# A trunk kernel's head reordered: the first eight projection tiles by column halves

## The chip, the cores and the metric

One NeuronCore of a Trainium2 chip runs the whole kernel. The metric is the device time of one execution in microseconds, median over several runs.

## The reference, cut to what matters

One layer of a streaming encoder, in float32, 1024 tokens of width 1024. The head of it is this:

```python
c_act = jax.nn.silu(c)
mod = (c_act @ w_ada[i] + b_ada[i]).reshape(bsz, N_MOD, D_MODEL)[:, :, None, :]
shift1, scale1, gate1 = mod[:, 0], mod[:, 1], mod[:, 2]
u = rms_norm(x, ln1[i]) * (1.0 + scale1) + shift1
# in mixer_sublayer
proj = u @ w_in          # 11296 columns; the first 2048 are the gates gl
gl, cb, cc, cx, z, xbc, dt = jnp.split(proj, split_at, axis=-1)
g_conv, g_ssm = jnp.split(jax.nn.sigmoid(gl), 2, axis=-1)
```

Behind it come a gated convolution, an SSD scan in eight groups, three output projections, a squared-ReLU MLP and a last RMSNorm. The change touches only the way to u and the first eight of the 88 column tiles of `w_in`.

## The kernel before, in words

Everything is held transposed: channels on the 128 partitions, tokens along the free dimension. x and u are eight blocks j of 128 channels, each in two halves h of 512 tokens (`xt[j][h]`, `uh[j][h]`, `ul[j][h]`). A product in float32 is made of three: an operand is split into a high part (a cast to the type fp32r on ScalarE) and a low part (the difference, on VectorE), and high x high, high x low and low x high are added up in PSUM (`mm3`, three matmuls of 128 x 128 by 128 x 512). A plain tile f of `w_in` (128 columns, all 1024 inputs) thus costs 2 x 8 x 3 = 48 matmuls. From some point on the tiles go in pairs through a Strassen form (`strassen_pair`) with 7 products of 12 matmuls, 84 for two tiles; it needs sums and differences of quarter blocks of u (`tops_of`), each split again.

The head goes in this order. `crow` (c as a row) and `prm` (all small parameters) are loaded; c is spread over the partitions by a product with ones, and silu gives `cb`. SP loads the left halves of x, the two `wada` tiles of block 0 (rows of `w_ada` for scale and shift), the right halves of x, and weights of `w_in` and further `wada` tiles in turn. ScalarE squares x, VectorE adds the squares, `st` collects column sums on TensorE, `rsqrt_eps` gives the root on VectorE, and a product of ones with a diagonal (`sdg`) spreads it over the partitions as `rb0` and `rb1`, for both halves before any u is made. Then for each block j VectorE forms shift and scale by two multiply-and-reduce instructions over 1024 columns (`gemv`, line 294), one column `s1c`, both halves of x times scale times `rb`, and both low parts; ScalarE makes the two high parts (`shift_split`, line 106). TensorE runs four tiles (0 to 3) over block j as soon as it is there, in all eight PSUM banks.

When all blocks are done, the four tiles are passed through tanh (`gl_evac`) and stored to `gl_d`; tiles 4 and 5 go plainly; VectorE and ScalarE form the Strassen operands; `dt` (a product with 64 columns, line 397) follows, and then the Strassen pairs (6, 7), (8, 9) to (14, 15), and the rest of the kernel. `dt_chain` and the remaining 32 gemvs (`wada2`, loaded by POOL into one buffer `wv`, three beside each pair) lie beside those pairs.

The order on each engine is made by a planner from its own model of durations, in the order of the program as priority, except where `issue_after` puts an instruction behind another. DMA issues stand in the instruction streams of SP, ScalarE and POOL.

Of the kernel before, what the change touches and what calls it, by code (L numbers as in the profile page):

```python
# [35 lines left out]
NPAR = DSK + 16  # L36


def hybrid_trunk(tc, xT, par, hrows, crow, wada1, wada2, win, wdt, wco, wso, wo, wup, wdt_, wdn, out):
# [26 lines left out]
    s1c = cp.tile([P, 8], F32, name="s1c")
    s2c = cp.tile([P, 8], F32, name="s2c")
    g1c = cp.tile([P, 8], F32, name="g1c")
    cp.tile([P, 24], F32, name="lpad")
# [193 lines left out]
    crw = glp.tile([1, T], F32, name="crw", tag="glt")  # L263
    sp.dma_start(crw, crow)
    sp.dma_start(prm, par)
    for h in (0, 1):
        ps = mm.tile([P, H], F32, name="mm")
        pe.matmul(ps, lhsT=ones[0:1, :], rhs=crw[:, hs[h]], start=True, stop=True)
        act.activation(ct[:, hs[h]], ps, AF.Tanh, scale=0.5)
        stt(cb[:, hs[h]], ct[:, hs[h]], 1.0, ps, ALU.add, ALU.mult)  # L270
# [9 lines left out]
    for h in (0, 1):  # L280
        for k in range(KT):
            sp.dma_start(xt[k][h], xT[k, :, hs[h]])
        if h == 0:
            load_ada(0)
    raws = [load_raw(win[f]) for f in (0, 1)]
    load_ada(1)
    raws.append(load_raw(win[2]))
    raws.append(p0.tile([P, T], F32, name='wx', bufs=1))
    sp.dma_start(raws[3], win[3])

    wps = mm.tile([P, H], F32, name="mm")
# [5 lines left out]
    def warm(n, x_):  # L297
        for _ in range(n):
            pe.matmul(wps, lhsT=ones, rhs=x_, start=True, stop=True)

    warm(4, xt[0][0])
# [1 line left out]
    for h in (0, 1):
        acc = None
        for k in range(KT):
            sq = p0.tile([P, H], F32, name="ssq" if k else "sacc", bufs=4 if k else 2)
            act.activation(sq, xt[k][h], AF.Square)
            if k:
                tt(acc, acc, sq, ALU.add)
            else:  # L310
                acc = sq
        for j in range(4):
            pe.matmul(st[:, 4 * h + j:4 * h + j + 1], lhsT=acc[:, j * P:j * P + P], rhs=ones[:, 0:1],
                      start=h == j == 0, stop=True, skip_group_check=True)
# [1 line left out]
    r = rsqrt_eps(p0, st[:, 0:8], 1.0 / T, [P, 8], "nst")
    rbs = []
    for h in (0, 1):
        dg = p0.tile([P, 4, P], F32, name="sdg", bufs=1)
        rdy = tt(dg, ident.unsqueeze(1).broadcast_to([P, 4, P]),  # L320
                 r[:, 4 * h:4 * h + 4].unsqueeze(2).broadcast_to([P, 4, P]), ALU.mult)
# [1 line left out]
        pe.matmul(ps, lhsT=ones, rhs=dg.rearrange("p j t -> p (j t)"), start=True, stop=True)
# [4 lines left out]
    ws = []
    sps = [[None, None] for _ in range(4)]
    for h in (0, 1):  # L330
        for f in range(4):
            pl, nm = (mm, "mm") if f < 2 else (ps0, ("sx", "st")[h])
            sps[f][h] = pl.tile([P, H], F32, name=nm)
    for j in range(KT):
        if j > 1:
            load_ada(j)
        if j in (0, 1):
            with tc.issue_after(rdy.ins), (tc.issue_after(rbc.ins) if j else contextlib.nullcontext()):
                for f in range(2):
                    ws.append(load_w(win[2 * j + f], raws[2 * j + f]))  # L340
        with tc.issue_after(rdy.ins) if j else contextlib.nullcontext():
            gemv(wa[j, 1], 8 + j)
            gemv(wa[j, 0], j)
        stt(s1c[:, j:j + 1], mcol[:, 8 + j:9 + j], 1.0, prm[:, LN1 + j:LN1 + j + 1], ALU.add, ALU.mult)
        for h in (0, 1):
            x_ = xt[j][h]
            stt(x_, x_, s1c[:, j:j + 1], rbs[h], ALU.mult, ALU.mult)
            rdy = shift_split(uh[j][h], ul[j][h], x_, mcol[:, j:j + 1])
        if j == 0:
            continue  # L350
        for jj in ((0, 1) if j == 1 else (j,)):
            for h in (0, 1):
                for f in range(4):
                    mm3([sps[f][h]], ws[f][0][:, jj * P:jj * P + P], ws[f][1][:, jj * P:jj * P + P],
                        [uh[jj][h]], [ul[jj][h]], jj == 0, jj == KT - 1)
# [721 lines left out]
```

## Time and profile before

| what | value |
|---|---|
| median of 3 runs | 2122.07 us (2121.62 to 2123.22) |
| profiled execution | 2126.34 us, its span 2124.3 us |
| granted TensorE clock, mean of the span | 0.989 |
| TensorE busy | 2089.6 us (98%) |
| VectorE busy | 1474.3 us (69%) |
| ScalarE busy | 927.4 us (44%) |
| POOL busy | 152.3 us (7%) |

Times in profile lines are in us from the span's start. A line of a timeline gives start, duration, engine, source line, operation, out<-in, count, and in brackets the idle time before it with what ended it. L is a line of the kernel; line 44 is any tensor-tensor operation, 47 any scalar-tensor-tensor, 89 a weight load, 96 a cast to a high part, 106 the high part of u, 113, 114 and 116 the three matmuls of `mm3`, 147 a matmul of a Strassen pair.

### The profile page before, as it was taken

The numbers are of one execution on the slowest core, as the hardware profiler recorded it, in microseconds if no ns is written. First come the engines' busy times: TensorE is split into PE (matmuls) and PEld (weight loads), VectorE is DVE, ScalarE is ACT, GpSimd is POOL, SyncE is SP. The second block draws the span as 40 slices with busy tenths as digits, with TensorE's granted clock in tenths as the row PEclk, the third lists the DMA queues.
The fourth block names the chain that finished last, engine by engine and source line by source line (L and its number), as shares of the span: only waits on it lengthen the run. The fifth ranks groups of instructions, "written<-read, shape, count | busy, mean of one in ns | idle before, by whom it ended". The sixth has DMA issues, their size and how long they took to land.

```text
span 2124.3 us, 26250 instructions
## 1 busy us (share of the span) xinstructions
PE 2089.6 (98%) x9776; PEld 1705.5 (80%) x9776; DVE 1474.3 (69%) x2278; ACT 927.4 (44%) x1554; POOL 152.3 (7%) x242
## 2 busy tenths in 40 slices
PE   7999999999999999999999999999999999999998
PEld 4778888888888887888877888888888888888887
DVE  7866888665786757576786558845866665668674
ACT  4433333224565636364664231233544454544432
POOL 0000000000000000000000000011000001232213
PEclk8999999999999999999999999999999999999998
DMA  8226554223133223232337586453144347988932
GB/s 302 80 100 200 189 189 165 71 80 122 60 100 110 85 90 85 95 115 80 104 121 262 189 299 201 159 203 124 65 164 159 145 162 261 304 241 254 275 77 80
DMA packets 133617, 327.32 MB, mean 154 GB/s; under 512 B 12481, under 2 KB 47681, under 8 KB 131954
## 3 DMA queue, kind: packets, MB, share of 16 engines
q1 hardware_dynamic: 98978, 202.76, 29.4%
q0 software_dynamic: 22240, 87.04, 12.9%
q10 hardware_dynamic: 12272, 35.85, 4.3%
q8 instruction: 77, 1.26, 0.2%
q14 instruction: 50, 0.41, 0.1%
HBM read 253.05 MB, written 72.55 MB: 153 GB/s over the span
## 4 chain that ended last, share of the span: by engine, by line
PE 82%; issue 10%; DVE 4%; DMA 2%; POOL 1%; ACT 1%; SPq 0%; DVEq 0%; POOLq 0%; ACTq 0%
PE mm L147 21%; PE mm L116 15%; PE mm L113 15%; PE mm L114 15%; PE mm L971 9%; PE B L603 2%; PE B L608 1%; PE C L625 1%; DMA wv<-in_wada 1%; DVE wada L294 1%; PE A L580 1%; DMA x<-in_xT 1%; POOL wv L418 1%; DVE ul L47 1%; DVE x L47 0%
## 5 line engine op out<-in xcount | busy, mean ns | idle before, releaser
L113 PE MATMUL mm<-uh,whi 128*128 128x512 f32 x768 | 303.0, 398 | 3.7 <-ACT uh L106 3.2
L114 PE MATMUL mm<-ul,whi 128*128 128x512 f32 x768 | 304.8, 397 | 0.0
L147 PE MATMUL mm<-t,whi 128*128 128x512 f32 x944 | 290.5, 390 | 0.9 <-DVE cq L44 0.9
L116 PE MATMUL mm<-uh,wlo 128*128 128x512 f32 x768 | 246.4, 396 | 1.9 <-DVE wlo L44 1.9
L96 ACT CAST whi<-wraw 128x1024 fp32r<-128x1024 f32 x101 | 106.1, 1050 | 261.9 <-PE mm L114 219.9
L44 DVE TENSOR_TENSOR wlo<-wraw,whi 128x1024 fp32r<-128x1024 f32 (+1 forms) x167 | 186.6, 1118 | 37.4 <-ACT whi L96 31.3
L147 PEld LDWEIGHTS mm<-t,whi 128*128 128x128 f32 x944 | 176.9, 188 | 39.1 <-DVE cq L44 2.4
L971 PE MATMUL mm<-op,whi 128*128 128x512 f32 x672 | 207.2, 389 | 1.0 <-DVE y L47 0.9
L147 PE MATMUL mm<-t,wlo 128*128 128x512 f32 x472 | 183.0, 389 | 0.0
L113 PEld LDWEIGHTS mm<-uh,whi 128*128 128x128 f32 x768 | 144.5, 189 | 35.6 <-ACT uh L106 4.9
L116 PEld LDWEIGHTS mm<-uh,wlo 128*128 128x128 f32 x768 | 144.9, 189 | 32.2 <-DVE wlo L44 2.3
L114 PEld LDWEIGHTS mm<-ul,whi 128*128 128x128 f32 x768 | 145.0, 189 | 29.4 <-issue 0.9
L113 PE MATMUL mm<-ys,whi 128*128 128x512 f32 x384 | 148.9, 397 | 2.3 <-DVE gt L47 1.8
L44 DVE TENSOR_TENSOR wlo<-s,whi 128x1024 fp32r<-128x1024 f32 (+1 forms) x114 | 112.0, 995 | 54.4 <-ACT whi L152 53.6
L114 PE MATMUL mm<-ys,whi 128*128 128x512 f32 x384 | 149.1, 396 | 0.0
L971 PEld LDWEIGHTS mm<-op,whi 128*128 128x128 f32 x672 | 126.0, 188 | 28.1 <-ACT whi L957 1.3
L47 DVE SCALAR_TENSOR_TENSOR cacc<-raw,hw,cacc 128x1024 f32<-128x1024 f32 x96 | 122.9, 1280 | 27.6 <-ACT cacc L555 27.2
L147 PE MATMUL mm<-s,whi 128*128 128x512 f32 x448 | 138.3, 389 | 0.7 <-ACT cu L170 0.7
L971 PE MATMUL mm<-op,wlo 128*128 128x512 f32 x336 | 130.7, 389 | 0.0
L597 ACT ACTIVATE seg<-acb,acum 128x128 f32<-128x128 f32 x256 | 81.9, 392 | 98.7 <-PE B L603 88.6
L47 DVE SCALAR_TENSOR_TENSOR y<-mm,mcol,y 128x512 f32<-128x512 f32 (+1 forms) x100 | 69.4, 706 | 77.6 <-PE mm L971 39.4
L116 PE MATMUL mm<-ys,wlo 128*128 128x512 f32 x384 | 122.5, 394 | 0.0
(280 smaller groups left out, 4080.9 us busy)
## 6 DMA issues: line engine op xcount, KB each, us to landing
wraw<-in_win SPq DMA_DIRECT2D x87, 512.0 KB, 3.5
dr<-in_wdt_ SPq DMA_DIRECT2D x108, 256.0 KB, 5.8
op_d<-hp POOLq DMA_DIRECT2D x12, 1792.0 KB, 6.0
hr<-op_d POOLq DMA_DIRECT2D x42, 512.0 KB, 6.3
wv<-in_wada POOLq DMA_DIRECT2D x32, 512.0 KB, 3.8
acb<-ac_d SPq DMA_DIRECT2D x64, 256.0 KB, 4.5
wraw<-in_wup SPq DMA_DIRECT2D x32, 512.0 KB, 3.5
gt<-gl_d SPq DMA_DIRECT2D x24, 512.0 KB, 4.4
```

The lines of the kernel that those rows point to most:

```text
L44: return eng.tensor_tensor(out=o, in0=a, in1=b, op=op)
L47: return dve.scalar_tensor_tensor(out=o, in0=a, scalar=s, in1=b, op0=op0, op1=op1)
L96: act.copy(hi, raw)
L113: pe.matmul(o, lhsT=wh, rhs=h_, start=start, stop=False)
L114: pe.matmul(o, lhsT=wh, rhs=l_, start=False, stop=False)
L116: last_mm[0] = pe.matmul(o, lhsT=wl, rhs=h_, start=False, stop=stop)
L147: last_mm[0] = pe.matmul(o, lhsT=l_[:, s_], rhs=r_, start=first and k == j == 0, stop=k == 3 and j == 2, skip_group_check=True)
L294: return dve.tensor_tensor_reduce(out=w_, in0=w_, in1=cb, scale=0.5, scalar=prm[:, BADA + o:BADA + o + 1], op0=ALU.mult, op1=ALU.add, accu ...
L418: pool.dma_start(w_, wada2[i])
L597: act.activation(seg[:, r, :], acb[:, r, :], AF.Relu, bias=acum[:, c, hd:hd + 1], scale=-1.0)
L603: pe.matmul(Bk[o:o + 64, P * (r // 2):P * (r // 2) + P], lhsT=xd[:, r, :], rhs=seg[:, r, :], start=True, stop=True, skip_group_check=True)
L971: pe.matmul(o, lhsT=l_[:, c_], rhs=t[:, r_, k, :], start=first and k == j == 0, stop=k == 3 and j == 2, skip_group_check=True)
```

## The change

The first eight tiles are now all plain ones (the Strassen pairs begin at tile 8), and the head runs by halves: left half of the tokens for all eight tiles, then the right half. The order of all instructions of the head on TensorE, ScalarE, VectorE and SP is the order of the program text: each is chained to the one before it on its engine. In detail:

- Left x, two small `wk` tiles, the weights of tiles 0 to 2, two blocks of `wada`, then right x are loaded by SP. `wk` holds the weights of scale and shift for block 0 transposed, so that these two columns come from TensorE (`first_col`, 8 one-column products each) instead of two gemvs; c itself comes as a column, `ccol`.
- Weights of tiles 3 to 7 are loaded by POOL as a raw buffer (three of them) comes free.
- The low parts of tiles 6 and 7 are made by ScalarE writing the negated raw tile and a DMA of POOL that adds the raw tile from memory.
- The sum of squares and the root of the right half are made between the steps of the left half (`square(1, k)`, `sums(1)`, `root(1)`).
- In the left half, a step j is: scale gemv, low part of block j-1, x times scale, shift gemv, high part of block j. Weight tiles join as they are ready and catch up on earlier blocks. In the right half the tiles 4 to 7 follow block by block, and then 0 to 3 one after the other.
- Tanh and store of gl go by halves. `wada` has 4 buffers instead of 8. `dt_chain` stands at pair 10 instead of 8, and the gemvs beside pairs 12 and 14 are four each instead of three beside 10, 12 and 14.

The diff, cut to its core:

```diff
+    block = nc.cur_bb.bb.instructions
+    head = len(block)
...
+    rows_c = [mm.tile([P, H], F32, name="mm") for _ in (0, 1)]
+    wps = mm.tile([P, H], F32, name="mm")
+    def warm(n):
+        for _ in range(n):
+            pe.matmul(wps[:, 0:P], lhsT=ones, rhs=ones, start=True, stop=True)
+    warm(3)
     for h in (0, 1):
...
+        pe.matmul(rows_c[h], lhsT=ones[0:1, :], rhs=crw[:, hs[h]], start=True, stop=True)
     xt = [[xk[k % 4].tile([P, H], F32, name=f"x{k}{h}") for h in (0, 1)] for k in range(KT)]
     wa = {}
+    def load_x(h):
+        for k in range(KT):
+            sp.dma_start(xt[k][h], xT[k, :, hs[h]])
     def load_ada(j):
         for q in (1, 0):
-            wa[j, q] = p0.tile([P, T], F32, name="wada", bufs=8)
+            wa[j, q] = p0.tile([P, T], F32, name="wada", bufs=4)
...
+    whs, wls, raws = [], [], []
+    def load_f(f):
+        raws.append(wp.tile([P, T], F32, name="wraw", bufs=3))
+        (sp if f < 3 else pool).dma_start(raws[f], win[f])
+        pl, nh, nl, n = (wp, "whi", "wlo", None) if f < 4 else (p0w, "whx", "wlx", None)
+        whs.append(pl.tile([P, T], F32R, name=nh, bufs=n))
+        wls.append(pl.tile([P, T], F32R, name=nl, bufs=n))
+    def high(f):
+        act.copy(whs[f], raws[f])
+    def low(f):
+        tt(wls[f], raws[f], whs[f].bitcast(F32), ALU.subtract)
+    def low_by_dma(f):
+        act.mul(wls[f], raws[f], -1.0)
+        pool.dma_start(wls[f], win[f], accum_op=ALU.add)
     def gemv(w_, o):
         return dve.tensor_tensor_reduce(out=w_, in0=w_, in1=cb, scale=0.5, scalar=prm[:, BADA + o:BADA + o + 1],
...
+    load_x(0)
+    wk = []
+    for q in (1, 0):
+        wk.append(p0w.tile([P, T], F32, name=f"wk{q}", tag="whx"))
+        sp.dma_start(wk[-1], wadak[:, q])
+    for f in range(3):
+        load_f(f)
+    load_ada(1)
+    load_ada(2)
+    load_x(1)
+    def first_col(n):
+        for k in range(KT):
+            pe.matmul(cps[:, n:n + 1], lhsT=wk[n][:, k * P:k * P + P], rhs=ccol[:, k:k + 1], start=k == n == 0,
+                      stop=k == KT - 1, skip_group_check=True)
+    accs = {}
+    def square(h, k):
+        sq = p0.tile([P, H], F32, name="ssq" if k else "sacc", bufs=2 if k else 1)
+        act.activation(sq, xt[k][h], AF.Square)
+        if k:
+            tt(accs[h], accs[h], sq, ALU.add)
+        else:
+            accs[h] = sq
+    def scale_of(j):
+        stt(s1c[:, j:j + 1], mcol[:, 8 + j:9 + j], 1.0, prm[:, LN1 + j:LN1 + j + 1], ALU.add, ALU.mult)
...
+    def sums(h):
         for j in range(4):
...
+            pe.matmul(st[:, 4 * h + j:4 * h + j + 1], lhsT=accs[h][:, j * P:j * P + P], rhs=ones[:, 0:1],
                       start=h == j == 0, stop=True, skip_group_check=True)
...
+    def root(h):
+        r = rsqrt_eps(p0, st[:, 4 * h:4 * h + 4], 1.0 / T, [P, 4], "nst")
+        dg = p0.tile([P, 4, P], F32, name="sdg", tag="ssq", bufs=2)
+        tt(dg, ident.unsqueeze(1).broadcast_to([P, 4, P]), r.unsqueeze(2).broadcast_to([P, 4, P]), ALU.mult)
+        return dg
+    def spread(dg):
...
         pe.matmul(ps, lhsT=ones, rhs=dg.rearrange("p j t -> p (j t)"), start=True, stop=True)
...
+        return ps
+    def keep_rb(ps):
+        rb = p0x.tile([P, H], F32, name=f"rb{len(rbs)}")
+        act.copy(rb, ps)
...
+    def scale_col(j):
+        gemv(wa[j, 1], 8 + j)
+        scale_of(j)
+    def scaled(j, h, rb=None):
+        x_ = xt[j][h]
+        stt(x_, x_, s1c[:, j:j + 1], rbs[h] if rb is None else rb, ALU.mult, ALU.mult)
+    def shift_hi(j, h):
+        act.activation(uh[j][h], xt[j][h], AF.Identity, bias=mcol[:, j:j + 1])
+    def shift_lo(j, h):
+        return stt(ul[j][h], xt[j][h], mcol[:, j:j + 1], uh[j][h].bitcast(F32), ALU.add, ALU.subtract)
+    sps = {}
+    def part(js, fs, h, kinds=(0, 1, 2)):
+        for f in fs:
+            if (f, h) not in sps:
+                pl, nm = (mm, "mm") if (f < 4) == (h == 0) else (ps0, "sx" if f % 4 < 2 else "st")
+                sps[f, h] = pl.tile([P, H], F32, name=nm)
+        for j in js:
+            for f in fs:
+                for i in kinds:
+                    w_, v_ = ((whs, uh), (whs, ul), (wls, uh))[i]
+                    pe.matmul(sps[f, h], lhsT=w_[f][:, j * P:j * P + P], rhs=v_[j][h], start=j == i == 0,
+                              stop=j == KT - 1 and i == 2, skip_group_check=True)
+    def gl_half(f, h):
+        t = glp.tile([P, T], F32, name="glt")
+        for i in (0, 1):
+            act.activation(t[:, hs[i]], sps[f + i, h], AF.Tanh, scale=0.5)
+            act.dma_start(gl_d[f + i][:, hs[h]], t[:, hs[i]])
+    rbs = []
+    warm(9)
+    act.activation(cc, prm[:, CCOL:CCOL + 8], AF.Tanh, scale=0.5)
+    stt(ccol, cc, 1.0, prm[:, CCOL:CCOL + 8], ALU.add, ALU.mult)
+    cps = mm.tile([P, H], F32, name="mm")
+    for k in range(KT):
+        square(0, k)
+    first_col(0)
     for h in (0, 1):
...
+        act.activation(ct[:, hs[h]], rows_c[h], AF.Tanh, scale=0.5)
+        stt(cb[:, hs[h]], ct[:, hs[h]], 1.0, rows_c[h], ALU.add, ALU.mult)
+    sums(0)
+    first_col(1)
+    high(0)
+    high(1)
+    dg = root(0)
+    for n, o in ((0, 8), (1, 0)):
+        stt(mcol[:, o:o + 1], cps[:, n:n + 1], 0.5, prm[:, BADA + o:BADA + o + 1], ALU.mult, ALU.add)
+    scale_of(0)
+    ps = spread(dg)
+    warm(8)
+    low(0)
+    scaled(0, 0, ps)
+    shift_hi(0, 0)
+    keep_rb(ps)
+    high(2)
+    load_f(3)
+    low(1)
+    load_f(4)
+    for j in range(1, KT):
+        scale_col(j)
+        shift_lo(j - 1, 0)
+        if j == 1:
+            for i in (0, 1, 2):
+                part((0,), (0, 1), 0, (i,))
+            part((0,), (2,), 0, (0, 1))
+        scaled(j, 0)
+        gemv(wa[j, 0], j)
+        if j == 1:
+            load_ada(3)
+            high(3)
+            part((0,), (3,), 0, (0, 1))
+            low(2)
+            part((0,), (2,), 0, (2,))
+            load_f(5)
+        shift_hi(j, 0)
+        if j == 1:
+            high(4)
+        if j == 2:
+            load_ada(4)
+            part((1,), range(3), 0)
+            part((1,), (3,), 0, (0, 1))
+            low(3)
+            part((0, 1), (3,), 0, (2,))
+            part((0, 1), (4,), 0, (0, 1))
+            load_f(6)
+            high(5)
+        if j == 3:
+            load_ada(5)
+            part((2,), range(4), 0)
+            part((2,), (4,), 0, (0, 1))
+            low(4)
+            part((0, 1, 2), (4,), 0, (2,))
+            part((0, 1, 2), (5,), 0, (0, 1))
+            load_f(7)
+            high(6)
+            low_by_dma(6)
+            square(1, 0)
+            square(1, 1)
+        if j == 4:
+            load_ada(6)
+            part((3,), range(5), 0)
+            part((3,), (5,), 0, (0, 1))
+            low(5)
+            part((0, 1, 2, 3), (5,), 0, (2,))
+            high(7)
+            low_by_dma(7)
+            for k in (2, 3):
+                square(1, k)
+            part((0, 1, 2, 3), (6,), 0, (0, 1))
+        if j == 5:
+            load_ada(7)
+            part((4,), range(6), 0)
+            part((4,), (6,), 0, (0, 1))
+            for k in (4, 5):
+                square(1, k)
+        if j == 6:
+            part((5,), range(6), 0)
+            part((5,), (6,), 0, (0, 1))
+            for k in (6, 7):
+                square(1, k)
+            sums(1)
+            part((0, 1, 2, 3, 4, 5), (6,), 0, (2,))
+            dg = root(1)
+        if j == 7:
+            keep_rb(spread(dg))
+            part((6,), range(7), 0)
+            part(range(7), (7,), 0)
+    shift_lo(7, 0)
+    part((7,), range(8), 0)
+    scaled(0, 1)
     for j in range(KT):
...
+        shift_hi(j, 1)
+        if j < KT - 1:
+            scaled(j + 1, 1)
+        rdy = shift_lo(j, 1)
+        if j < 4:
+            gl_half(2 * j, 0)
+        part((j,), range(4, 8), 1)
+    for f in (0, 2):
+        for f_ in (f, f + 1):
+            part(range(KT), (f_,), 1)
+    last_of = {}
+    pinned = {e_.engine for e_ in (pe, act, dve, sp)}
+    for i_ in block[head:]:
+        if i_.engine in pinned:
+            if i_.engine in last_of:
+                tc.add_manual_dep(i_, last_of[i_.engine].name, mybir.DependencyInfo(
+                    mybir.DependencyClass.NoSync, mybir.DependencyReason.DATA))
+            last_of[i_.engine] = i_
+    for f in (4, 6, 0, 2):
+        gl_half(f, 1)
...
+    p0w.release()
...
-    ws = [load_w(win[f]) for f in (4, 5)]
     tks, X = [], {n: [] for n in ("11", "21", "22", "T1", "T2", "T3", "T4")}
...
@@ -381,9 +538,6 @@
...
@@ -446,16 +600,16 @@
...
-    for f in range(6, 16, 2):
+    for f in range(8, 16, 2):
         ts_ = [glp.tile([P, T], F32, name="glt") for _ in (0, 1)]
         def gl_ev(i, h, src):
...
-        if f == 8:
+        if f == 10:
             dt_chain()
-        elif f > 8:
-            gemvs(3)
+        elif f > 10:
+            gemvs(4)
...
         for i in (0, 1):
...
@@ -1037,7 +1191,7 @@
...
+        cols(np.repeat(a["d_skip"][0], 64)), cols(a["c"]),
...
     for f in range(8):
@@ -1055,6 +1209,7 @@
...
+        "wadak": np.stack([wada[:, 1024 * q:1024 * q + P].reshape(8, P, P) for q in (0, 1)]).transpose(2, 0, 1, 3).reshape(P, 2, D),
...
```

More of the change, by code (lines that the diff above doesn't have):

```diff
@@ L35, with hybrid_trunk @@
 DSK = BADA + 48
-NPAR = DSK + 16
-def hybrid_trunk(tc, xT, par, hrows, crow, wada1, wada2, win, wdt, wco, wso, wo, wup, wdt_, wdn, out):
+CCOL = DSK + 16
+NPAR = CCOL + 8
+def hybrid_trunk(tc, xT, par, hrows, crow, wada1, wadak, wada2, win, wdt, wco, wso, wo, wup, wdt_, wdn, out):
     nc = tc.nc
@@ L58, in hybrid_trunk @@
     mm = tc.alloc_tile_pool(name="mm", bufs=4, space=PSUM)
-    prm = cp.tile([P, NPAR], F32, name="prm")
+    s1c, s2c, g1c, cc = [cp.tile([P, 8], F32, name=n) for n in ("s1c", "s2c", "g1c", "cc")]
     ident = cp.tile([P, P], F32, name="ident")
@@ L64, in hybrid_trunk @@
     onec = cp.tile([P, P], F32R, name="onec")
+    prm = cp.tile([P, NPAR], F32, name="prm")
     mcol = cp.tile([P, 48], F32, name="mcol")
[L66 to L69, printed above, removed]
+    ccol = cp.tile([P, 8], F32, name="ccol")
     dcs = cp2.tile([P, 64], F32, name="dc")
@@ L263, in hybrid_trunk @@
     crw = glp.tile([1, T], F32, name="crw", tag="glt")
+    block = nc.cur_bb.bb.instructions
+    head = len(block)
     sp.dma_start(crw, crow)
     sp.dma_start(prm, par)
+    rows_c = [mm.tile([P, H], F32, name="mm") for _ in (0, 1)]
[4 more added lines that the diff above has]
+    warm(3)
     for h in (0, 1):
[L267 to L270, printed above, removed]
+        pe.matmul(rows_c[h], lhsT=ones[0:1, :], rhs=crw[:, hs[h]], start=True, stop=True)
     xt = [[xk[k % 4].tile([P, H], F32, name=f"x{k}{h}") for h in (0, 1)] for k in range(KT)]
     wa = {}
+    def load_x(h):
+        for k in range(KT):
+            sp.dma_start(xt[k][h], xT[k, :, hs[h]])
     def load_ada(j):
         for q in (1, 0):
-            wa[j, q] = p0.tile([P, T], F32, name="wada", bufs=8)
+            wa[j, q] = p0.tile([P, T], F32, name="wada", bufs=4)
             sp.dma_start(wa[j, q], wada1[j, :, q])
[L280 to L291, printed above, removed]
+    whs, wls, raws = [], [], []
[12 more added lines that the diff above has]
+        pool.dma_start(wls[f], win[f], accum_op=ALU.add)
     def gemv(w_, o):
@@ L295, in gemv @@
                                         op0=ALU.mult, op1=ALU.add, accum_out=mcol[:, o:o + 1])
[L297 to L301, printed above, removed]
-    st = ps0.tile([P, H], F32, name="st")
[L303 to L311, printed above, removed]
+    load_x(0)
@@ L312, in hybrid_trunk @@
+    def scale_of(j):
+        stt(s1c[:, j:j + 1], mcol[:, 8 + j:9 + j], 1.0, prm[:, LN1 + j:LN1 + j + 1], ALU.add, ALU.mult)
+    st = ps0.tile([P, H], F32, name="st")
+    def sums(h):
         for j in range(4):
-            pe.matmul(st[:, 4 * h + j:4 * h + j + 1], lhsT=acc[:, j * P:j * P + P], rhs=ones[:, 0:1],
+            pe.matmul(st[:, 4 * h + j:4 * h + j + 1], lhsT=accs[h][:, j * P:j * P + P], rhs=ones[:, 0:1],
                       start=h == j == 0, stop=True, skip_group_check=True)
-    warm(2, acc)
@@ L316, in hybrid_trunk @@
[L316 to L321, printed above, removed]
+    def root(h):
[3 more added lines that the diff above has]
+        return dg
@@ L334, in hybrid_trunk @@
-    for j in range(KT):
[L335 to L355, printed above, removed]
@@ L357, in gl_evac @@
-    def gl_evac(f, ps):
-        t = glp.tile([P, T], F32, name="glt")
-        for h in (0, 1):
-            act.activation(t[:, hs[h]], ps[h], AF.Tanh, scale=0.5)
-        act.dma_start(gl_d[f], t)
-    for f in range(4):
-        gl_evac(f, sps[f])
+    def scale_col(j):
[6 more added lines that the diff above has]
+        act.activation(uh[j][h], xt[j][h], AF.Identity, bias=mcol[:, j:j + 1])
@@ L383, in hybrid_trunk @@
         xk[k].release()
-    for f in (4, 5):
-        gl_evac(f, proj(ws[f - 4], uh, ul))
     p0d = tc.alloc_tile_pool(name="p0d", bufs=1, reuse_waits="tile")
```

9 lines of the change are left out of this document (1 added, 8 removed).

## The prediction

> **What bounds it now.** First the page: TensorE is the bound almost everywhere, so a change to the head is worth what it moves the instant at which TensorE's unbroken run begins.
>
> ```profile
> PE 2089.6 (98%) x9776; PEld 1705.5 (80%) x9776; DVE 1474.3 (69%) x2278; ACT 927.4 (44%) x1554; POOL 152.3 (7%) x242
> ```
>
> Then the busy time by stage (sum, then PE, PEld, DVE, ACT, POOL, granted clock, DMA share, GB/s).
>
> ```profile
> 10.00:15.00 5.00, 2.98 (x9) 1.30 (x7) 4.61 (x8) 2.06 (x4) 0.00 (x0) 0.94 1.04 399
> 20.00:25.00 5.00, 3.81 (x11) 2.78 (x12) 2.63 (x12) 2.09 (x2) 0.00 (x0) 0.50 1.02 408
> 40.00:45.00 5.00, 5.00 (x24) 4.05 (x23) 4.87 (x9) 1.39 (x2) 0.00 (x0) 1.00 0.53 179
> 86.00:89.00 3.00, 3.00 (x9) 2.29 (x9) 3.00 (x5) 2.11 (x5) 0.00 (x0) 0.52 0.91 329
> 153.00:200.00 47.00, 47.00 (x209) 38.94 (x208) 34.91 (x50) 16.84 (x24) 4.98 (x9) 1.00 0.58 195
> ```
>
> In 40 to 45 us TensorE and VectorE are both full: one input block costs TensorE 24 matmuls and VectorE as long. In 86 to 89 us, after a stall, the clock is 0.52. After that TensorE is full to the end (the waits of TensorE from 130 to 420 us add up to the one row below). So I compare one mark in both kernels. Its rows, from the timeline of TensorE:
>
> ```profile
> 33.39 1.22 PE L113 MATMUL mm<-uh,whi 128*128 128x512 f32 x2 [3.19 <-ACT uh L106]
> 107.39 0.40 PE L397 MATMUL st<-uh,wd 128*64 128x512 f32 x1
> 119.93 0.55 PE L147 MATMUL mm<-uh,whi 128*128 128x512 f32 x1 [0.95 <-ACT cu L170]
> 123.67 0.40 PE L147 MATMUL mm<-uh,whi 128*128 128x512 f32 x1
> 132.53 0.39 PE L147 MATMUL mm<-uh,whi 128*128 128x512 f32 x1
> 140.01 0.39 PE L147 MATMUL mm<-uh,whi 128*128 128x512 f32 x1
> 140.46 0.61 PE L147 MATMUL mm<-t,whi 128*128 128x512 f32 x2
> PE mm L147 <- DVE cq L44: 0.9, 2, 0.7
> ```
>
> 33 matmuls lie between the starts at 132.53 and 140.01: 0.2267 us each at full clock. That run on uh and ul is three products of 12, the third already of pair (8, 9); the pair (6, 7) still owes 12. So at 140.46 TensorE has done 288 matmuls of plain tiles 0 to 5, 84 of one pair, and dt: **the mark is 140.5**. dt with its gap and slow stretch is 107.39 to 123.67 less the 17 pair matmuls that fill it (6, 2 and 9 between these rows; 3.9 us): 12.4 us. The new kernel stands at the same mark when it has done 384 matmuls (8 x 48: 12 more, 2.7 us) and dt. Work alone would be 87.0 + 12.4 = 99.4 us, so a start at 24 without stalls would put the mark at 123.4, a gain of 17. The question is the stalls.
>
> **The start of the new head.** Rows for it, from the timelines:
>
> ```profile
> 12.27 1.28 DVE L294 CUSTOM_DVE_ANT_0 wada<-wada,cb,prm 128x1024 f32<-128x1024 f32 x1 [0.18 <-DMA wada<-in_wada]
> 2.39 3.75 PE L268 MATMUL mm<-crw,ones 1*128 1x512 f32 x4 [2.39 <-DMA crw<-in_crow]
> 21.19 1.86 PE L313 MATMUL st<-ones,sacc 128*128 128x1 f32 x8 [5.24 <-DVE sacc L44]
> 23.09 0.17 DVE L50 TENSOR_SCALAR nst<-st 128x8 f32<-128x8 f32 x1 [1.96 <-PE st L313]
> 25.37 0.69 DVE L44 TENSOR_TENSOR sdg<-ident,nst 128x512 f32<-128x512 f32 x1
> 26.47 1.82 PE L323 MATMUL st<-sdg,ones 128*128 128x512 f32 x2
> 29.08 1.12 PE L323 MATMUL st<-sdg,ones 128*128 128x512 f32 x2 [0.79 <-DVE sdg L44]
> ```
>
> The first wk tile takes the place in SP's queue that the first wada tile has, behind prm and the left half of x: landed at 12.3. One first_col is 8 one-column products; the trace has 4 of them (x8 records) in 1.86 at half clock, so 3.5 for one, estimated 1.8 at full clock. TensorE runs first_col(0), sums(0), first_col(1), spread in that order. At half clock: 12.3 + 3.5 = 15.8, sums to 17.6, the root (23.09 to 25.37, 2.3) and sdg (0.7) on VectorE to 20.7, first_col(1) to 21.1, spread 1.8 to 22.9. At full clock throughout: 14.1, 15.0, 18.0, then low(0) on VectorE ends last, 19.7. So VectorE begins scaled(0) at S = 19.7 to 23.0. I take 22.0, nearer the slow end: the filler matmuls run out by about 10 (two rows products to 6.1, nine quarter-size warm products after them), and before, the granted clock was 0.94 over 10 to 15, where TensorE's work paused, and 0.50 over 20 to 25. The old gemvs of block 0 (2 x 1.21) go from VectorE.
>
> **The left half on VectorE.** Rows of one step of before, from the timelines of VectorE and ScalarE, and of the other operations:
>
> ```profile
> 58.88 1.28 DVE L294 CUSTOM_DVE_ANT_0 wada<-wada,cb,prm 128x1024 f32<-128x1024 f32 x1
> 60.09 1.28 DVE L294 CUSTOM_DVE_ANT_0 wada<-wada,cb,prm 128x1024 f32<-128x1024 f32 x1
> 61.29 0.15 DVE L47 SCALAR_TENSOR_TENSOR s1c<-mcol,prm 128x1 f32<-128x1 f32 x1
> 61.48 1.42 DVE L47 SCALAR_TENSOR_TENSOR x<-x,s1c,rb 128x512 f32<-128x512 f32 x2
> 62.27 1.39 ACT L106 ACTIVATE uh<-x,mcol 128x512 fp32r<-128x512 f32 x2 [4.09 <-DVE x L47]
> 28.94 2.35 DVE L44 TENSOR_TENSOR wlo<-wraw,whi 128x1024 fp32r<-128x1024 f32 x2
> 15.67 5.47 DVE L44 TENSOR_TENSOR sacc<-sacc,ssq 128x512 f32<-128x512 f32 x7 [0.23 <-ACT ssq L307]
> 30.72 1.05 ACT L96 CAST whi<-wraw 128x1024 fp32r<-128x1024 f32 x1
> 31.67 1.05 ACT L96 CAST whi<-wx 128x1024 fp32r<-128x1024 f32 x1
> 14.25 0.63 ACT L307 ACTIVATE sacc<-x 128x512 f32<-128x512 f32 x1 [2.78 <-DMA x<-in_xT]
> ```
>
> From start to start: gemv 1.21, s1c 0.19, a 512-wide multiply-add 0.66 (two end after 1.42), low 1.14, an accumulation 0.70 to 0.79, uh 0.67, a cast 0.95, a square 0.63. One step j is two gemvs, s1c, shift_lo and scaled: 3.93. Up to the low part of block 6, VectorE does: scaled(0) 0.66; low 1 to 5, 5.7; steps 1 to 6, 23.6; 7 accumulations, 5.3; root and sdg, 3.0; gemv, s1c and shift_lo(6), 2.1: 40.4 us of work.
>
> Its waits come from the written order, in which both engines are tied: an accumulation stands behind its square, and the square on ScalarE behind shift_hi(j), which needs the second gemv of step j (start g). uh starts at g + 1.4. At j = 3 ScalarE then does uh 0.67, cast 0.95, the negated copy 0.95 (taken as a cast; it has no row of that size), two squares 1.2: ready at g + 5.2. VectorE is there after gemv and low, g + 2.35: it waits 2.9. At j = 4 one square less: 2.3. At j = 5 and 6 (no cast, no low) 1.6 each. Before root(1) it waits for sums(1) on TensorE: 1.9 with 0.3 of handing over, 2.2. Sum 10.6. So shift_lo(6) ends at 22.0 + 40.4 + 10.6 = 73.0.
>
> **TensorE.** Behind that low part stand, in order, 21 matmuls of block 6 (three for each of seven tiles), 21 of tile 7 on blocks 0 to 6, and 24 of block 7 (its low part is ready by about 77): 66 x 0.2267 = 15.0, left half done at 88.0. The other 126 (28.6 us) fit before it even at half clock for a third of the time. The right half is 192 matmuls, 43.5 us: VectorE needs 16 x 0.66 there, ScalarE 8 x 0.67 and the tanhs; banks come free before TensorE asks. 131.5. Plus dt 12.4: **mark 143.9 against 140.5, +3.4 us**.
>
> **Edits costed at nothing.** The Strassen operands of x and wd move under the right half. Their rows:
>
> ```profile
> 75.32 2.49 DVE L44 TENSOR_TENSOR x<-x,x 128x512 f32<-128x512 f32 x4
> 94.51 4.29 DVE L44 TENSOR_TENSOR t<-x,t 128x512 fp32r<-128x512 f32 x7
> 97.02 0.33 SPq L389 DMA_DIRECT2D wdr<-in_wdt  x1
> 99.06 0.41 ACT L391 CAST wd<-wdr 128x256 fp32r<-128x256 f32 x1 [0.68 <-DMA wdr<-in_wdt]
> ```
>
> VectorE needed 23.5 for the operands (75.3 to 98.8). It is free at about 99, done at 123, and wd's load and two casts take 3: 126, 5 ahead of TensorE's 131.5. If that cover goes, each us counts. The 16 half-size gl stores on ScalarE's queue (8 full ones before) lie in the same 43 us. SP loses five weight loads and stands at ada(3) for its buffer with nothing but ada tiles behind it. POOL gets five loads and two accumulating ones; POOL stands at each for a free wraw buffer or the negated copy, and only other such loads stand behind. Rows of loads from POOL (issue to landing; the last two are of the tiles wv and hr):
>
> ```profile
> wlo<-in_wdt_ POOLq DMA_DIRECT2D x36, 256.0 KB, 7.3
> DMA to landing us min/median/max: 3.6/3.8/5.3
> DMA to landing us min/median/max: 3.7/6.3/12.0
> ```
>
> Tile 6's low part is asked for at about 41 and used at 66, tile 7's at 50 and 78: hidden at 7.3 doubled. Raw tile 6 is asked for when low(3) is done, 34, and cast at 39: 4.6 of room; raw tile 3 has 5.1 (22 to 27). I take 3.8 to 4.5, the wv rows (same size, same source kind), so no wait. Four gemvs in each of two pairs instead of three:
>
> ```profile
> 162.69 1.28 DVE L294 CUSTOM_DVE_ANT_0 wv<-wv,cb,prm 128x1024 f32<-128x1024 f32 x1 [1.74 <-DMA wv<-in_wada]
> 168.23 1.28 DVE L294 CUSTOM_DVE_ANT_0 wv<-wv,cb,prm 128x1024 f32<-128x1024 f32 x1 [0.78 <-DMA wv<-in_wada]
> ```
>
> 5.5 apart, 22 in a pair of 84 matmuls (19.0): 6 us too long over two pairs, made up under the z pairs (16.5 in 19.0). Cover: VectorE has 12 idle us in 153 to 200. Bounds 0 to 6; I take 0, since such waits cost TensorE 0.9 in 290 us.
>
> **Base.** The profiled run took 2126.34 (span 2124.3); the median is 2122.07. I add +3.4 to the median: **2125.5**. About 0.2% (4.2 us) is what a measurement here tells from no change.
>
> [...] A TensorE that waits is slowed for a stretch: 0.52 in 86 to 89. I count none in the last 66 matmuls. [...]
>
> **Rivals.**
> 1. Faster: the accumulations find their squares ready, because ScalarE, by the walk above, is idle for some 5 us a step before shift_hi and could do them there. Then the 10.6 go: 2114.9. It decides when the waits sum to under 3. Against it: the order is chained on both engines, and squares are written after shift_hi.
> 2. Raw tiles late on POOL's queue, like hr. At 7.0 raw tile 6 is 2.4 late and tile 3 about 1: +3.4, 2128.9; at 9 about 2133. It decides above 5 us of landing. For it: behind the first wk tile SP's queue holds 6.3 MB up to the end of x, at the 0.4 MB/us of 20 to 25 until about 28. [...]
> 3. TensorE slowed three times at the left half's end, each time like 86 to 89 (0.48 of 3 us lost, 1.4): +4.3, 2129.8.
> 4. The gemvs' overhang or late Strassen operands reach TensorE: up to +6, 2131.5.
>
> **Chances.** Forecast 0.55 (its own range 2122 to 2127.5: S from 19.7 to 23.0, sums at full clock -1, one slowed stretch +1.4), rival 1 0.15, rival 2 0.14, rivals 3 and 4 0.08 each. The forecast's centre lies 0.8 under the 0.2% line, so it gives faster 0.02, same 0.34, slower 0.19; rival 1 gives faster 0.12, same 0.03; the others same 0.05, slower 0.25. Sum: 0.14, 0.42, 0.44. Range 2116 to 2132.
>
> **What would show it.** First matmul on uh near 24; VectorE idle behind squares near 40, 49, 57 and 64; TensorE's left half done near 88, and the first matmul on wd near 131.5. Wrong if TensorE ends the left half by 80 (rival 1), if high parts wait for loads (2), or if TensorE waits after 145 (4).

## The result, and the profile after

The change makes the kernel slower: 2134.61 us median (2133.95 to 2136.44) against 2122.64 (four runs of the kernel before; the three of the table above gave 2122.07), ratio 1.0056 [1.0038, 1.0073]. Two further measurements of the same program (below) give 2133.56 and 2134.55. So it costs about 11 us, where +3.4 was forecast, and the time lies outside the range. The profiled execution took 2133.95 us, its span is 2132.2. TensorE, from the page of after:

```profile
PE 2094.7 (98%) x9848; PEld 1715.8 (80%) x9848; DVE 1463.6 (69%) x2275; ACT 927.9 (44%) x1554; POOL 156.9 (7%) x249
```

VectorE has 10.7 us less to do than before, and still the span is longer. Where it stands in the left half, from the timeline of VectorE of after (bracket: idle time before the instruction, and what ended it):

```profile
22.73 0.75 DVE L48 SCALAR_TENSOR_TENSOR x<-x,s1c,st 128x512 f32<-128x512 f32 x1 [0.42 <-PE st L358]
45.15 0.69 DVE L45 TENSOR_TENSOR sacc<-sacc,ssq 128x512 f32<-128x512 f32 x1 [5.35 <-ACT ssq L334]
52.98 1.49 DVE L45 TENSOR_TENSOR sacc<-sacc,ssq 128x512 f32<-128x512 f32 x2 [2.07 <-ACT ssq L334]
59.70 1.49 DVE L45 TENSOR_TENSOR sacc<-sacc,ssq 128x512 f32<-128x512 f32 x2 [1.31 <-ACT ssq L334]
66.43 1.49 DVE L45 TENSOR_TENSOR sacc<-sacc,ssq 128x512 f32<-128x512 f32 x2 [1.31 <-ACT ssq L334]
69.06 0.16 DVE L51 TENSOR_SCALAR nst<-st 128x4 f32<-128x4 f32 x1 [1.14 <-PE st L347]
73.23 0.74 DVE L48 SCALAR_TENSOR_TENSOR ul<-x,mcol,uh 128x512 fp32r<-128x512 f32 x1
```

The reader sees the five waits that the forecast named, at the places that it named; they sum to 11.2 us. TensorE's marks, from its timeline: the first matmul of the right half, the first on wd, and the first on t in a run whose place is used below.

```profile
88.87 0.39 PE L391 MATMUL mm<-uh,whx 128*128 128x512 f32 x1
132.39 0.40 PE L551 MATMUL st<-uh,wd 128*64 128x512 f32 x1
164.93 0.62 PE L146 MATMUL mm<-t,whi 128*128 128x512 f32 x2
```

TensorE's waits from 130 to 420 us, for after:

```profile
PE mm L146 <- DVE cq L45: 3.9, 6, 1.4
PE mm L146 <- ACT cu L169: 0.9, 1, 0.9
```

Before lost 0.9 us to cq there. Against after, the first matmul on A (a stage behind all projection pairs) moves from 543.1 to 552.1:

```profile
L580 PE MATMUL A<-cf,bf x128: 270/274/377, 543.1 to 1194.3; 128*128 128x128 f32 x128
```

```profile
L734 PE MATMUL A<-cf,bf x128: 270/274/377, 552.1 to 1200.8; 128*128 128x128 f32 x128
```

The profiled execution of before lay 4 us above its median, so one more execution of each kernel was traced.

### The profile page after: what moved, and what is told of

Same layout as the page of the kernel before. It is cut to its first block, busy times and chain, and to the rows that moved or that the text cites. A ratio compares the mean times of both kernels' runs of the same rounds, so it can differ in the third digit from the quotient of the medians.

```text
span 2132.2 us, 26414 instructions
## 1 busy us (share of the span) xinstructions
PE 2094.7 (98%) x9848; PEld 1715.8 (80%) x9848; DVE 1463.6 (69%) x2275; ACT 927.9 (44%) x1554; POOL 156.9 (7%) x249
## 4 chain that ended last, share of the span: by engine, by line
PE 78%; issue 15%; DVE 3%; DMA 3%; POOL 1%; ACT 0%; SPq 0%; DVEq 0%; POOLq 0%; ACTq 0%
PE mm L146 18%; PE mm L113 13%; PE mm L112 13%; PE mm L115 13%; PE mm L1125 11%; PE mm L391 1%; PE B L757 1%; DMA wraw<-in_win 1%; PE B L762 1%; PE C L779 1%; PE st L391 1%; PE sx L391 1%; POOL wv L572 1%; DMA x<-in_xT 1%; DVE wada L311 1%
## 5 line engine op out<-in xcount | busy, mean ns | idle before, releaser
L146 PE MATMUL mm<-t,whi 128*128 128x512 f32 x912 | 280.9, 390 | 3.9 <-DVE cq L45 3.9
L113 PE MATMUL mm<-ul,whi 128*128 128x512 f32 x704 | 278.7, 396 | 0.0
L112 PE MATMUL mm<-uh,whi 128*128 128x512 f32 x704 | 278.7, 396 | 0.0
L115 PE MATMUL mm<-uh,wlo 128*128 128x512 f32 x704 | 223.2, 395 | 0.0
L95 ACT CAST whi<-wraw 128x1024 fp32r<-128x1024 f32 x96 | 100.8, 1050 | 261.1 <-PE mm L113 220.9
L146 PEld LDWEIGHTS mm<-t,whi 128*128 128x128 f32 x912 | 170.7, 188 | 41.8 <-DVE cq L45 6.5
L146 PE MATMUL mm<-t,wlo 128*128 128x512 f32 x456 | 176.9, 389 | 0.0
L115 PEld LDWEIGHTS mm<-uh,wlo 128*128 128x128 f32 x704 | 132.2, 188 | 27.2 <-issue 0.2
L113 PEld LDWEIGHTS mm<-ul,whi 128*128 128x128 f32 x704 | 132.3, 188 | 26.7 <-issue 0.9
L112 PEld LDWEIGHTS mm<-uh,whi 128*128 128x128 f32 x704 | 132.3, 188 | 26.5 <-issue 0.2
```

Source lines behind the costliest of these rows:

```text
L95: act.copy(hi, raw)
L112: pe.matmul(o, lhsT=wh, rhs=h_, start=start, stop=False)
L113: pe.matmul(o, lhsT=wh, rhs=l_, start=False, stop=False)
L115: last_mm[0] = pe.matmul(o, lhsT=wl, rhs=h_, start=False, stop=stop)
L146: last_mm[0] = pe.matmul(o, lhsT=l_[:, s_], rhs=r_, start=first and k == j == 0, stop=k == 3 and j == 2, skip_group_check=True)
```

## The experiments

**1. Both kernels again.** 

> The kernel before once more, for a second trace of it: the first profiled execution lies 4 us above its median, so part of the 12 us between the medians may be missing in the comparison of the traces (7.9 us at the end of the span). Expected median 2122 to 2125 and the same waits behind the head (under 2 us of TensorE for cq between 145 and 400). If the first trace of before had lost its 4 us ahead of 145, the first matmul on t would come earlier than 124.4 here; if behind, the first A matmul or the first sdg product of the last stages would.

> The changed kernel once more, unchanged, as the base of the experiments beside it. Both theories expect a ratio near 1.0056 to the kernel before (+12 us), TensorE's left half done near 88.9 us and 3 to 4 us of TensorE waits on VectorE between 130 and 420 us.

Before: 2124.81, ratio 1.0 [0.999, 1.001]. The change: 2133.56, ratio 1.005 [1.0035, 1.0064]. The second trace of before has its first matmul on A at 541.5 and waits for cq of 0.7; that of the change at 552.4 and 3.2. So most of the 11 us is there by the A stage, and what varies behind it (as a wait of TensorE of 2.4 us for gt between 1200 and 1400 that the change's first trace has and its second has not) is not the change's.

**2. The gemvs beside the pairs put back.**

```
-        if f == 10:
+        if f == 8:
             dt_chain()
-        elif f > 10:
-            gemvs(4)
+        elif f > 8:
+            gemvs(3)
```

> Only the placing of dt_chain (beside pair 8 again) and of the gemvs (three beside pairs 10, 12, 14) is undone; the head stays as changed. If the four gemvs a pair make VectorE late, TensorE's waits on cq between 130 and 420 us fall from 3.9 to about 0.9 and the time falls by about 3 us against the changed kernel. Rival: these waits come from the head's end shifting against the loads, whatever the number a pair; then they stay within 1 us and so does the time.

2134.55, ratio 1.0054 [1.0039, 1.0069]: no gain. The planner in fact gives both programs the same order of instructions on every engine. They share one buffer, and each load into it waits for the gemv on the load before, as the brackets of POOL's loads in after show:

```profile
183.63 0.55 POOL L572 DMA_DIRECT2D wv<-in_wada  x1 [5.49 <-DVE mcol L311]
189.04 0.53 POOL L572 DMA_DIRECT2D wv<-in_wada  x1 [4.86 <-DVE mcol L311]
```

These two loads are 5.4 us apart; over all 32 (177.59 to 374.99) it is 6.4 in the mean, whatever number the program text puts beside a pair. This part of the change is no change. Its trace (cq 5.0, A at 554.7) is a third sample of the change.

**3. Squares early.** ScalarE squares the right half ahead of the high part, VectorE's accumulations stay where they are.

```
+        if 3 <= j <= 6:
+            square(1, 2 * j - 6)
+            square(1, 2 * j - 5)
         shift_hi(j, 0)
 ...
-            square(1, 0)
-            square(1, 1)
+            add_square(1)        # and add_square(k) at the three other places
```

> Only the order on ScalarE is changed: the squares of the right half stand ahead of shift_hi(j) in steps 3 to 6, and the accumulations stay where they are on VectorE. Theory of the chained waits: VectorE's waits for squares (5.4, 2.1, 1.3, 1.3 us) go, TensorE becomes the next wait before the root, the left half ends near 82 instead of 88.9, and the time falls by 6 to 7 us against the changed kernel. Rival, weights late on POOL's queue: the 5.4 was the raw tile's lateness and comes back as a wait of TensorE for tile 6 or of the high parts; then less than 3 us is won. Rival, work behind the head decides: nothing is won.

2125.05, ratio 1.0008 [0.9996, 1.002]; once more 2124.86, 1.0004 [0.9992, 1.0015]. That is 9 us below the change, more than the 6 to 7 expected. Its VectorE accumulates without a wait and TensorE begins the right half 9.2 us sooner:

```profile
45.48 1.48 DVE L45 TENSOR_TENSOR sacc<-sacc,ssq 128x512 f32<-128x512 f32 x2
```

```profile
79.65 0.39 PE L398 MATMUL mm<-uh,whx 128*128 128x512 f32 x1
```

The waits behind squares are shown to be on the path. In this version the raw tile is off it: ScalarE still waits for raw tile 6, to 42.13, but nothing of VectorE stands behind that any more.

**4. Block 0 by gemvs, three ways.** First in the wada buffers:

```
-    wk = []
...
-        sp.dma_start(wk[-1], wadak[:, q])
+    load_ada(0)
...
-    first_col(0)
...
+    gemv(wa[0, 1], 8)
     sums(0)
-    first_col(1)
...
     dg = root(0)
...
+    gemv(wa[0, 0], 0)
```

> Only the first conditioning products are taken back from TensorE: the two wada tiles of block 0 are loaded in the place of wk and multiplied on VectorE, the first beside sums(0), the second behind the root. Theory of the chained waits: scaled(0) starts 2 us earlier (20.3 to 20.9 instead of 22.7), but the raw tiles from POOL's queue and the squares hold VectorE back to where it was, so the left half ends within 0.5 us of 88.9 and the time stays within 1 us. Rival, the slow start of the head costs what was lost: the time falls by 2 us or more.

2127.96, ratio 1.0019 [1.001, 1.0028]: my theory (within 1 us) falls. But the gain isn't in the head: the right half begins at 88.5, against 88.9, although VectorE begins scaled(0) 2.2 us sooner. SP's queue in this version shows one reason. Its loads of blocks 1 and 2 take 10 us to issue, 8.3 of them in waits for VectorE to free a wada buffer, and right x stands behind them:

```profile
9.70 10.07 SPq L289 DMA_DIRECT2D wada<-in_wada  x4
19.82 4.29 SPq L284 DMA_DIRECT2D x<-in_xT  x8
```

With the two tiles in wk's buffers (`p0w.tile(..., tag="whx")`) instead:

> The change with block 0 by two gemvs in wk's buffers, the squares where the change has them. Theory (in the change VectorE's chain sets the end of the left half, so a start 2.2 us earlier passes through): low part of block 6 near 71.0 instead of 73.2, first right-half matmul near 86.7 instead of 88.9, time 2129 to 2131.5, according to whether TensorE's waits for cq behind the head shrink as in the run with block 0 in the wada buffers. Rival (raw tile 6 is cast when it lands, at 42, whatever the start): first right-half matmul at 88 to 89, and the time that of the change, 2133 to 2135, or, if only the waits behind the head count, 2128.

2128.95, ratio 1.0022 [1.0013, 1.0031], and the right half at 89.4: the start is given back in the head even so (theory wrong there), and the gain is again behind it. scaled(0) begins 2.0 us sooner than in after. ScalarE shows where the first 0.9 go: raw tile 6 comes only 1.1 us sooner (first the row of this version, then that of after).

```profile
40.99 1.04 ACT L301 CAST whx<-wraw 128x1024 fp32r<-128x1024 f32 x1 [2.85 <-DMA wraw<-in_win]
```

```profile
42.08 1.05 ACT L301 CAST whx<-wraw 128x1024 fp32r<-128x1024 f32 x1 [2.65 <-DMA wraw<-in_win]
```

The 1.1 us last to the end of VectorE's left half: the multiply of block 7 (scaled(7)) begins at 72.81, against 73.89. There TensorE's granted clock falls (third number from the end), which it doesn't in after; rows of 72 to 77 us of this version and of after:

```profile
72.00:77.00 5.00, 4.36 (x13) 3.27 (x12) 4.34 (x11) 1.20 (x3) 0.00 (x0) 0.66 0.00 0
```

```profile
72.00:77.00 5.00, 4.30 (x16) 2.99 (x17) 4.33 (x9) 1.12 (x2) 0.00 (x0) 1.00 0.01 3
```

A third of 5 us is about 1.7, more than the 1.1 that were left.

Then with the early squares, first in the wada buffers, then in wk's:

> The two edits together: squares of the right half ahead of the high part, and block 0 by two gemvs instead of the one-column products. With the squares early TensorE had no waits over 0.6 us between 32 and 58 us, so a start 2.2 us earlier (scaled(0) at 20.5 instead of 22.7) should reach the end of the left half whole. Theory (the start counts once the waits for squares are gone): first matmul on wd near 121 instead of 123.2, time 2121 to 2123, 2 to 4 us below the squares alone. Rival 1 (the 5.6 us that block 0 by gemvs gave alone lie behind the head, whatever the head does): about 2119.5. Rival 2 (loads of raw tiles now hold the left half): no earlier wd, 2124 to 2125.

> Squares early and block 0 by two gemvs, but with the two block-0 tiles in the buffers that wk had, so that SP's queue doesn't stand for 10 us at the third block's tiles as it did when block 0 took two of the four wada buffers. Theory (the start was given back because SP stood, and x and the next tiles came later): scaled(0) at 20.5, first right-half matmul near 77.4 (79.6 with the squares alone), first matmul on wd near 121, time 2120.5 to 2122.5. Rival (the raw tiles on POOL's queue hold the left half at fixed times): first right-half matmul stays at 79 to 80, time 2123 to 2125.

2123.25, 0.9992 [0.9982, 1.0002], with the right half only at 82.7 (SP's queue stands for 10 us here too), and **2119.0, 0.9979 [0.9969, 0.999]**; once more 2119.49, 0.9985 [0.9972, 0.9998]. This last version beats both kernels, the one before by 3 to 5 us. Its right half begins at 79.94 in the first trace and at 78.20 in the second, against 79.65 and 79.69 with the squares alone. The two differ by a fall of the clock at the left half's end (last section), so the first alone looks as if the loads held the left half at fixed times, as the rival says; the second has 1.5 us of the start left. The rival is wrong on the time as well. In the first trace TensorE has no wait for cq at all in 130 to 420 us:

```profile
PE mm L146 <- ACT cu L169: 0.9, 1, 0.9
```

**5. The root of the right half later** (`root(1)` behind shift_lo(6), the seven tiles of block 6 ahead of the spread, block 7 ahead of tile 7).

> Squares early and the root of the right half behind the low part of block 6, block 0 as in the change. Theory (VectorE's wait for the sums and the root are on the path once the squares are early): first right-half matmul near 77.2 instead of 79.6, time 2122 to 2123.5. Rival (TensorE full, or its clock falls in the new place): 79 to 80, time 2124 to 2126.

> As the run before, and the root of the right half stands on VectorE behind the low part of block 6 instead of ahead of it, with the seven tiles of block 6 ahead of the spreading product on TensorE, and block 7 ahead of tile 7. Theory (with the squares early, VectorE's 2.2 us of waiting for the sums and 2.9 us of root are what the left half's end waits for): another 2 to 2.5 us off the left half, first right-half matmul near 75, time 2118 to 2120, 4 to 6 us faster than the kernel before. Rival (TensorE is full there and only shifts its work): as the run without it, 2120.5 to 2122.5.

2123.93, 0.9997 [0.9988, 1.0007], and 2121.74, 0.9989 [0.9978, 1.0]. The right half begins at 78.8 and 78.2. That is 0.9 and 1.7 us sooner and not 2 to 2.5, and the second trace of the fastest version begins it at 78.2 without this edit. The time does not follow: against the same kernels without this edit (2125.05 and 2119.0) one is lower and one higher, with intervals that overlap.

**6. Behind the head: 8 gemvs moved** ahead of the dt product, into VectorE's idle stretch, with two buffers of their own.

```
+    gem = iter(range(32))
+    for _, i in zip(range(8), gem):
+        w_ = p0d.tile([P, T], F32, name="wv0", bufs=2)
+        pool.dma_start(w_, wada2[i])
+        gemv(w_, 16 + i)
...
-        elif f > 10:
-            gemvs(4)
```

The stretch in after (VectorE's timeline), and TensorE's waits from 130 to 420 us with the edit:

```profile
144.99 1.29 DVE L45 TENSOR_TENSOR s<-wraw 128x512 f32<-128x512 f32 x2 [21.36 <-PE st L558]
```

```profile
PE mm L146 <- ACT cu L169: 2.5, 1, 2.5
PE mm L146 <- DVE cq L45: 1.2, 3, 0.7
```

> Change as it is, but 8 of the 32 gemvs beside the pairs run ahead of the dt product, where VectorE stands idle for 21.4 us (123.6 to 145.0), from two buffers of their own; the pairs (12, 13) and (14, 15) then have none. Theory (VectorE comes out of the head behind: it is idle while TensorE finishes the right half and then late with sums and cq in 145 to 400): TensorE's waits for cq, 3.2 to 5.0 us so far, fall under 1.5, time 2130.5 to 2132. Rival (the waits come from the order inside a pair, not from VectorE's load, as moving gemvs between pairs gave nothing): 2133.5 to 2134.6, waits of 3 us or more.

> Squares early, block 0 by gemvs and 8 gemvs ahead of the dt product, all three. If the three causes (waits for squares in the left half, the slow start, VectorE behind after the head) are separate: 1.5 to 2.5 us below the first two together, 2119 to 2121, so 2.5 to 4.5 us faster than the kernel before. If VectorE's load behind the head is no cause: 2121 to 2123, like the two together.

2132.98, 1.0034 [1.0022, 1.0046], between the two ranges, and with the other two edits 2126.15, 1.0002 [0.9991, 1.0013], above both ranges and 3 us above the two edits without it. The waits for cq fall as expected, but 1.6 us of it comes back as a longer wait for cu; the sum is at best 1 us.

**7. Why block 0 by gemvs gains behind the head.** Behind the head the order of instructions is the same on every engine in the change and its two versions with block 0 by gemvs, and again in the squares alone and the fastest version. Four runs ask whether it is the place or the source of the inputs, or the products:

> The fastest version, with one more DMA of 4 KB at the start that reads 8 columns of the input wadak, so that this input is read by the kernel as in the change. Theory (where the inputs lie in memory decides how gemv loads and z stores land behind the head, and an input that is not read takes no place): waits for cq of 2 us or more and 2121.5 to 2125, like the squares alone. Rival (the place of the inputs is the same in both, the waits come from something else): as the control, within 1.5 us.

> The change with no instruction altered, only the input wadak placed behind all other inputs instead of between wada1 and wada2. Theory (the place of the inputs): waits for cq under 1.5 us, time 2127 to 2130.5. Rival: 2133 to 2135.5 and waits of 3 us or more, like the change.

> Squares early, block 0 by one-column products, but the two wk tiles are loaded from wada1 (block 0's rows) instead of wadak, so shift and scale of block 0 are computed from other weights; the instructions are the same as with the squares alone. Theory 1 (the source of the load decides): 2119 to 2121.5, as with block 0 by gemvs. Theory 2 (the products on TensorE and the later start decide): 2123.5 to 2126, as with the squares alone.

> The fastest version (squares early, block 0 by two gemvs in wk's buffers) with 16 further one-column products of ones at the places where the change has its own; their result is not used. The first products delay the sums of squares, so scaled(0) starts near 22.5 instead of 20.5. Theory 1 (the source of the load decides): 2118.5 to 2121, the later start again absorbed in the left half. Theory 2 (the products and the later start decide): 2123 to 2125.5.

| version | ratio to before | cq waits in its trace, us |
|---|---|---|
| fastest version, again | 0.9985 [0.9972, 0.9998] | 0.6 |
| the same, reads some of wadak | 0.9978 [0.9968, 0.9989] | 2.3 |
| the same, with 16 products | 0.9993 [0.9982, 1.0005] | 6.9 |
| squares early, again | 1.0004 [0.9992, 1.0015] | 5.7 |
| the same, wk from wada1 | 1.0006 [0.9997, 1.0015] | 4.2 |
| the change, wadak last | 1.0032 [1.0022, 1.0043] | 3.0 |

> The fastest version so far once more (squares early, block 0 by two gemvs in wk's buffers), as the control for the next run and to see whether its 2119.0 stands: 2117.5 to 2121 expected, TensorE's waits for cq between 145 and 400 under 1 us.

> The squares alone once more, as the control on the same chip: 2123 to 2126, waits for cq behind the head of 1.5 us or more.

The source of the load is out (wk from wada1: as with the squares alone; that kernel takes other weights for block 0's shift and scale, so it serves for the time alone). Reading wadak is out. Placing wadak last gave 2130.75, 3 to 4 us under the change, between the two theories and with intervals that overlap, and its waits for cq stayed. The products added to the fastest version (2122.83) lie between it and the squares alone, and overlap both, though the uh matmuls began as early as without them (22.7), so the later start that this run was to bring as well did not come. The waits for cq differ between executions of one kernel, too: with the squares alone 2.7 and 5.7 us, in executions of 2121.79 and 2130.73. So one trace of each version can't decide, and what makes the waits likelier with the products stays open.

## Why the prediction was wrong

**The head: right, nearly to the us.** scaled(0) began at 22.73 (forecast 22.0). VectorE's waits sum to 11.2 (10.6), with 5.35, 2.07, 1.31, 1.31 and 1.14 for the 2.9, 2.3, 1.6, 1.6 and 2.2 written down: too little by 2.4 at the first, too much at each of the others. shift_lo(6) began at 73.23 (end forecast 73.0), the right half at 88.87 (88.0), the matmuls on wd at 132.39 (131.5). Rival 1 was rightly set aside, and the squares early show that the chain in the written order is what holds it.

**POOL's loads: the size was off, and the cost hidden in the first wait.** I took 3.8 to 4.5 us from issue to landing, from the wv rows. Raw tile 6 was issued at 35.28 and cast at 42.08, 6.8 us later:

```profile
35.28 0.53 POOL L295 DMA_DIRECT2D wraw<-in_win  x1 [4.78 <-DVE wlo L45]
```

Rival 2 was right on the landing (its case at 7.0). Its 2.4 us are those by which the first wait is longer; the smaller waits behind it gave 1.9 of them back. No run here shows what made the landing longer; the DMA engines were at a share of 0.96 in 30 to 35 us of after and of 0.84 in 35 to 40.

**The mark: this step failed.** It says that before has done 84 matmuls of one pair at 140.46. The matmuls of pairs up to there, from the groups of the Strassen line in that window:

```profile
L147 PE MATMUL mm<-t,whi x24: 389/389/389, 124.4 to 132.1; 128*128 128x512 f32 x24
L147 PE MATMUL mm<-uh,whi x20: 388/389/628, 106.5 to 140.0; 128*128 128x512 f32 x20
L147 PE MATMUL mm<-ul,whi x20: 387/389/628, 106.7 to 140.2; 128*128 128x512 f32 x20
L147 PE MATMUL mm<-uh,wlo x19: 389/389/628, 106.9 to 139.8; 128*128 128x512 f32 x19
L147 PE MATMUL mm<-t,wlo x12: 389/389/389, 125.7 to 132.3; 128*128 128x512 f32 x12
```

That is 95, 11 more. The pair (6, 7) does owe 12, as the forecast says: its last product is on t, and VectorE adds it to cu (the buffer of a pair's first product) at 143.38. But of the three products in the run on uh and ul from 132.53, two belong to the pair (8, 9) and not one (the last of their 24 matmuls runs later). ScalarE's copy to cu, which follows the first product of each pair, comes for the second time at 135.45, as soon as the first product of that run has ended. ScalarE's two copies, and VectorE's addition:

```profile
119.28 0.59 ACT L170 COPY cu<-mm 128x512 f32<-128x512 f32 x1
135.45 0.59 ACT L170 COPY cu<-mm 128x512 f32<-128x512 f32 x1 [4.16 <-PE mm L147]
```

```profile
143.38 0.69 DVE L44 TENSOR_TENSOR cu<-mm,cu 128x512 f32<-128x512 f32 x1 [0.19 <-PE mm L147]
```

So the walk of the new kernel was set against a mark that already held 11 more matmuls: 11 x 0.2267 = 2.5 us. Counted rightly the same walk gives +5.9. The walk itself was right: the change has done the same 95 pair matmuls at 164.93, which less 95 x 0.2267 is 143.4, forecast 143.9. At that place before has 84 matmuls more still to do than the change, so the two stand 164.93 - 140.46 - 84 x 0.2267 = +5.4 apart in the profiled executions, and 165.6 - 139.75 - 19.0 = +6.8 in the means of the traces (three of the change: 164.93, 165.05, 166.77; two of before: 140.46, 139.04).

**Edits costed at nothing: this failed too, and by more.** The forecast took the waits for cq at what before has, 0.9 us. VectorE is late with cq by 3.2 to 5.0 us in three traces of the change (mean 4.0) against 0.7 and 0.9 before: +3.2. That is rival 4's sign, TensorE waiting after 145. Its reason falls in part: four gemvs a pair instead of three are the same program. The cover that I named (VectorE's idle time in 153 to 200) does not help, as VectorE idles 21.4 us ahead of the pairs, and then stands for the load at half of the 32 gemvs. Its waits in 100 to 400 us, of after and then of before:

```profile
DVE wv L311 <- DMA wv<-in_wada: 31.3, 16, 3.2
DVE s L45 <- PE st L558: 21.4, 1, 21.4
```

```profile
DVE wv L294 <- DMA wv<-in_wada: 29.5, 18, 3.2
DVE s L44 <- PE st L404: 19.1, 1, 19.1
```

Before has nearly the same of both and is not late, so they do not say why the change is. That cause stays open.

**The sum.** +6.8 at the mark and +3.2 behind are 10.0 of the 10.8 us by which the first matmul on A moves (mean 553.1 against 542.3); 0.8 stays without a place. Of the 7.4 us that the forecast lacks there, 2.5 are the count at the mark and 3.2 the waits for cq; the rest is 0.7 between the two traces of before, 0.2 of the walk and the 0.8.

**The clock.** Rival 3 did not take place at the end of the change's left half, where the clock was 1.00 in every 5 us from 55 to 90. The forecast has a TensorE that waits slowed for a stretch. After has such a stretch behind TensorE's wait of 5.20 us that ends at 47.96, behind the first of the five waits (0.57 in 45 to 50, 0.75 in 50 to 55), and none behind its wait of 1.79 us that ends at 63.30 (1.00 in 60 to 65). As TensorE waits for VectorE there once more, the slow stretch cost nothing. In versions of experiment 4 a fall at the left half's end did take place (0.66 in 5 us), and cost some 1.7 us.

## What to carry to other kernels

A mark that compares two kernels is a count of work: check it against the groups of the trace in that window before a time hangs on it. Where two engines are chained to a written order, put the producer ahead of the step that makes it late: moving the squares took back 9 us here. A wait that is small in one kernel (0.9 us for cq) can't be carried over to another whose order differs. And a start won early can be lost on the way: of 2.0 us, 1.1 were left at the end of VectorE's left half, and one fall of the clock took those.
